# Layer 1's sums of squares for the sub-norm as two rounded products instead of one fp32 product

## The chip, the core and the metric

One core of a Trainium2 chip runs the whole program. The time is the device time of one execution in microseconds (us). The core has five engines that each work through a queue of their own in order: PE (TensorE, matrix products into PSUM), DVE (VectorE), ACT (ScalarE), POOL (GpSimd, which works on SBUF) and SP (SyncE, which here only issues transfers). They wait for each other by semaphores.

## What is computed

The program is a trunk of two layers over 2048 tokens with a width of 1024. Layer 0 has two attention mixers, layer 1 one differential attention with eight heads of width 128. The change lies in layer 1, behind the attention of a head:

```python
o = differential_attention(q1, q2, k1, k2, v, lam)
o = rms_norm(o, subln_g) * (1.0 - lambda_init)
y = (o.reshape(b, s, C_W) * jax.nn.silu(gate)) @ w_out
return x + y
```

with

```python
def rms_norm(x, g):
    xf = x.astype(jnp.float32)
    y = xf * lax.rsqrt(jnp.mean(xf * xf, axis=-1, keepdims=True) + EPS)
    return (y * g.astype(jnp.float32)).astype(x.dtype)
```

So for every token and head the 128 values of `o` are squared and summed, and the row is scaled by the inverse root of their mean.

## The kernel before

Every large product works with rounded operands (type `F32R` in the source; the trace calls it fp32r on what is written and f32 on what is read). A value is split into a high part, a copy into `F32R` on ACT, and a low part, the difference, on DVE or POOL; a product of two split operands is then three products (`mm3`, lines 214 to 216).

The kernel runs layer 0's projections (tiles named `p0...`), its mixing (`m...`), layer 1's projections (`p1...`), and layer 1's mixing (`c...`, `_mix1`). Layer 1's mixing takes the four blocks of 512 queries from the last to the first, and in each block the eight heads: 32 passes in all. I count them 0 to 31; heads 0 to 7 are block 3, heads 24 to 31 block 0. A pass has these parts:

- `scores` (line 880): products of queries and keys (`cS`, lines 901 and 902), a maximum on DVE (905), the exponential on ACT (908), then on POOL, and for every fifth chunk on DVE, the two softmaxes are scaled and joined (924 to 934).
- `values` (line 937): for each 128 keys, transposes of the probabilities on PE (`ctr`, 947), the split on ACT and DVE (950, 951), and three products into `cO` (954 to 956).
- `gate` (line 965), at the end of a head's values: SP loads the gate's values `g` (969), ACT copies the head's output out of PSUM into `o` (971) and squares it into `sq` (973), ACT makes the first two steps of the sigmoid from `g` into `sg` (975, 976), POOL multiplies `o` by `g` (977).
- `rest` (line 979), put off: it is kept in the list `normal` and run when the values of the next head have reached `kt == 2` (lines 957 to 959), for the last head by `leave`. PE sums the squares over the head's 128 values, which lie on the partitions, with a matrix of ones (`ms`, 981); ACT takes the logarithm (982), DVE joins it with the sigmoid's (983), ACT takes the exponential (984), DVE scales `o` (985). In blocks 3 and 0 `o` is split for the output projection at once (`split`, lines 1002 and 1003); in blocks 2 and 1 it goes out to memory (989) and is read back by `fetch` (1013).

Next to the heads runs the work of `side`: the products for the gates (`cG`), and the output projection of each finished block (`com`, `out_step`). `pace` weaves these streams together in the order in which the source issues them. From this the framework makes each engine's queue at build time with a planner: an instruction is put into its engine's queue when, in the planner's own reckoning, its inputs are there and its buffer is free, the earlier issued first. On the chip each queue is then worked through in that order.

A buffer comes from a pool by its tag: tiles with the same tag share a fixed number of places. Tag "g" of pool `sb` has two places (`bufs=2`); "sq" and "sg" have one each. The PSUM pool `ptr` has two places under tag "tr", for the transposes `ctr` and for `ms`.

Of the kernel before, what the change touches and what calls it, by code (L numbers as in the profile page):

```python
# [11 lines left out]
F32R = mybir.dt.float32r  # L12
AF = mybir.ActivationFunctionType
ALU = mybir.AluOpType
# [4 lines left out]
P = 128  # L19
# [4 lines left out]
BLK = NTB * P  # L24
# [7 lines left out]
def f32(ap):  # L32
    return ap.bitcast(F32)
# [52 lines left out]
class Trunk:  # L86
# [758 lines left out]
    def _mix1(self, es):  # L845
        nc, tc, a, s = self.nc, self.tc, self.a, self.s1
        n = "c"
# [8 lines left out]
        sb = pool("sb", 2)  # L856
# [5 lines left out]
        mm = nc.tensor.matmul  # L862
# [74 lines left out]
        def values(h, b, res):  # L937
            us = res["u"]
            O = pO.tile([P, BLK], F32, tag="O", name=n + "O")
            nkt = (b + 1) * NTB  # L940
            for kt in range(nkt):
                j0 = max(0, kt - b * NTB)
                wd = (NTB - j0) * P
                tp = ptr.tile([P, 512], F32, tag="tr", name=n + "tr")
                kk = (kt % 4) * P
                for j in range(j0, NTB):
                    nc.tensor.transpose(tp[:, (j - j0) * P:(j - j0 + 1) * P], us[j][kt // 4][:, kk:kk + P], self.ident)  # L947
                H = sb.tile([P, 512], F32R, tag="ptH", name=n + "ptH", bufs=3)
                L = sb.tile([P, 512], F32R, tag="ptL", name=n + "ptL", bufs=3)
                nc.scalar.activation(H[:, :wd], tp[:, :wd], AF.Copy)  # L950
                nc.vector.tensor_tensor(L[:, :wd], tp[:, :wd], f32(H[:, :wd]), ALU.subtract)  # L951
                o = O[:, j0 * P:]
                vH, vL = (v[:, kk:kk + P] for v in res["v"][kt // 4])
                mm(o, vH, H[:, :wd], start=(kt == 0), stop=False, skip_group_check=True)
                mm(o, vL, H[:, :wd], start=False, stop=False, skip_group_check=True)
                mm(o, vH, L[:, :wd], start=False, stop=(kt == nkt - 1), skip_group_check=True)  # L956
                if kt == 2:
                    while normal:
                        normal.pop(0)()
                yield wd / P  # L960
            gate(h, b, O)
# [3 lines left out]
        def gate(h, b, O):  # L965

            rows, tok = slice(h * P, (h + 1) * P), slice(b * BLK, (b + 1) * BLK)
            g = sb.tile([P, BLK], F32, tag="g", name=n + "gg")
            nc.sync.dma_start(g, s["g"][rows, tok])
            o = ot.tile([P, BLK], F32, tag="ot", name=n + "ot")  # L970
            nc.scalar.activation(o, O, AF.Copy)
            sq = sb.tile([P, BLK], F32, tag="sq", name=n + "sq", bufs=1)
            nc.scalar.activation(sq, o, AF.Square)
            sg = sb.tile([P, BLK], F32, tag="sg", name=n + "sg", bufs=1)
            nc.scalar.activation(sg, g, AF.Exp, scale=-1.0)
            nc.scalar.activation(sg, sg, AF.Ln, bias=self.one)
            nc.gpsimd.tensor_tensor(o, o, g, ALU.mult)

            def rest():
                ms = ptr.tile([P, BLK], F32, tag="tr", name=n + "ms")  # L980
                mm(ms, f32(self.ones), sq, start=True, stop=True)
                nc.scalar.activation(sq, ms, AF.Ln, bias=self.eps, scale=1.0 / P)
                nc.vector.scalar_tensor_tensor(sg, sq, 0.5, sg, ALU.mult, ALU.add)
                nc.scalar.activation(sg, sg, AF.Exp, scale=-1.0)
                nc.vector.scalar_tensor_tensor(o, o, self.sub, sg, ALU.mult, ALU.mult)
                if b in (0, NB - 1):
                    split(h, b, o)
                else:
                    nc.sync.dma_start(s["o"][rows, tok], o)
                ended.add((h, b))  # L990

            normal.append(rest)
# [7 lines left out]
        def split(h, b, o):  # L1000
            yH, yL = y_tile(b), y_tile(b)
            nc.scalar.activation(yH, o, AF.Copy)
            nc.gpsimd.tensor_tensor(yL, o, f32(yH), ALU.subtract)
            y[b][h] = yH, yL
# [214 lines left out]
```

## Time and profile before

| | |
|---|---|
| median of 3 runs | 2887.84 us (2879.25 to 2898.03) |
| profiled execution | 2891.3 us |
| its span, first to last instruction | 2889.4 us |
| mean granted PE clock | 0.979 |
| layer 1's mixing, from the first `gate` to the last | 1883.7 to 2853.7 us |

The profile is one execution. Times in it are microseconds from the span's start unless marked ns. A group row reads: line, engine, operation, output tile `<-` input tiles, shapes, `x` count, busy time in us, mean of one in ns, idle time of the engine just before, and what ended that idle time. A row of a tile or a source line reads: count, then shortest, median and longest duration in ns, then first and last start. A row of the chain reads: start, duration, engine, tile and line, and how many pieces were joined. A row of the timeline adds, in brackets, how long the engine had been idle before and what released it. PEld is the load of a product's fixed operand, which overlaps PE's products. Products are pipelined and their ends are modelled, so the distance from one start to the next says more of their cost than the duration of one.

### The profile page before, as it was taken

How to read it: one execution, taken by the hardware profiler on the slowest of the kernel's cores; microseconds unless marked ns; L12 is line 12 of the kernel's file. 1: busy time of each engine (PE TensorE's matmuls, PEld its weight loads, DVE VectorE, ACT ScalarE, POOL GpSimd, SP SyncE). 2: the span in 40 equal slices, each digit the busy share in tenths (PEclk: the TensorE clock that was granted, in tenths of full speed). 3: DMA queues.
4: the chain of work that ended last, by engine and by line, in shares of the span. 5: the costliest groups of instructions: out<-in, count | busy, mean ns of one | idle time of the engine just before them, and what ended most of it. 6: DMA issues, size and time to landing. Idle time of an engine off the chain costs nothing.

```text
span 2889.4 us, 45239 instructions
## 1 busy us (share of the span) xinstructions
PE 2709.6 (94%) x13704; PEld 2234.1 (77%) x13704; DVE 1955.8 (68%) x4874; ACT 1592.5 (55%) x4135; POOL 1588.1 (55%) x1740
## 2 busy tenths in 40 slices
PE   7999999998999998999999999989999999899898
PEld 5888888887788887777788887767777877677677
DVE  7752385257888885598638852667777888888742
ACT  4443543367676674343343322657667777777753
POOL 3541251335544453367645741667777887887841
PEclk9999999999999999999999999999999999999999
DMA  5673344649987874557884454776777787668772
GB/s 161 222 244 135 117 137 131 201 117 241 238 202 174 199 186 120 212 201 246 268 291 153 125 185 155 229 203 178 209 213 217 209 230 216 174 188 217 211 248 92
DMA packets 408868, 555.86 MB, mean 192 GB/s; under 512 B 47152, under 2 KB 187184, under 8 KB 408624
## 3 DMA queue, kind: packets, MB, share of 16 engines
q1 hardware_dynamic: 408624, 552.96, 65.4%
q8 instruction: 110, 1.80, 0.3%
q14 instruction: 134, 1.10, 0.1%
HBM read 388.18 MB, written 164.63 MB: 191 GB/s over the span
## 4 chain that ended last, share of the span: by engine, by line
PE 66%; DVE 11%; DMA 8%; ACT 4%; issue 3%; POOL 2%; SPq 1%; ACTq 0%; DVEq 0%; POOLq 0%
PE p1mm L216 5%; PE p1mm L214 5%; PE p1mm L215 5%; PE cS L901 3%; PE cS L902 3%; PE p0mm L216 3%; PE p0mm L215 3%; PE p0mm L214 3%; PE ctr L947 3%; PE cG L214 2%; PE cO L956 2%; PE com L214 2%; PE cG L215 2%; PE mom L214 2%; PE cG L216 2%
## 5 line engine op out<-in xcount | busy, mean ns | idle before, releaser
L908 ACT ACTIVATE cP<-cS,cnm 128x512 f32<-128x512 f32 (+3 forms) x640 | 398.7, 629 | 156.1 <-DVE cnm L905 99.2
L905 DVE TENSOR_REDUCE cnm<-cS 128x1 f32<-128x512 f32 (+3 forms) x640 | 374.8, 599 | 90.3 <-PE cS L902 86.1
L924 POOL TENSOR_SCALAR cP<-cP,crl,ce 128x512 f32<-128x512 f32 (+3 forms) x288 | 213.7, 755 | 248.8 <-DVE crl L919 74.5
L901 PE MATMUL cS<-ck,cqd 128*128 128x512 f32 (+3 forms) x640 | 263.0, 415 | 44.5 <-ACT cP L908 22.4
L215 PE MATMUL p1mm<-p1wL,p1hH 128*128 128x512 f32 x768 | 302.0, 393 | 0.4 <-POOL p1wL L310 0.4
L214 PE MATMUL p1mm<-p1wH,p1hH 128*128 128x512 f32 x768 | 301.7, 394 | 0.7 <-ACT p1wH L308 0.7
L216 PE MATMUL p1mm<-p1wH,p1hL 128*128 128x512 f32 x768 | 302.0, 394 | 0.0
L310 POOL TENSOR_TENSOR p0wL<-p0ws,p0wH 128x512 fp32r<-128x512 f32 (+1 forms) x124 | 149.0, 1232 | 270.5 <-ACT p0wH L308 260.5
L934 POOL TENSOR_TENSOR cP<-cP,cP 128x512 f32<-128x512 f32 (+3 forms) x256 | 288.6, 1148 | 0.5
L214 PE MATMUL p0mm<-p0wH,p0hH 128*128 128x512 f32 (+1 forms) x640 | 239.5, 376 | 4.7 <-ACT p0vt L472 3.3
L310 POOL TENSOR_TENSOR p1wL<-p1ws,p1wH 128x512 fp32r<-128x512 f32 x128 | 168.6, 1336 | 136.4 <-ACT p1wH L308 129.5
L902 PE MATMUL cS<-ck,cql 128*128 128x512 f32 (+3 forms) x640 | 236.5, 374 | 6.8 <-DMA cql<-qL 6.8
L216 PE MATMUL p0mm<-p0wH,p0hL 128*128 128x512 f32 (+1 forms) x640 | 239.6, 375 | 1.0 <-DVE p0hL L336 1.0
L215 PE MATMUL p0mm<-p0wL,p0hH 128*128 128x512 f32 (+1 forms) x640 | 239.2, 374 | 0.0
L951 DVE TENSOR_TENSOR cptL<-ctr,cptH 128x512 fp32r<-128x512 f32 (+1 forms) x320 | 190.3, 598 | 49.3 <-ACT cptH L950 48.5
L950 ACT ACTIVATE cptH<-ctr 128x512 fp32r<-128x512 f32 (+1 forms) x320 | 170.0, 538 | 57.8 <-PE ctr L947 57.4
L901 PEld LDWEIGHTS cS<-ck,cqd 128*128 128x128 f32 x640 | 123.2, 193 | 86.0 <-ACT cP L908 53.6
L933 POOL TENSOR_SCALAR cP<-cP,crl,ce 128x512 f32<-128x512 f32 (+3 forms) x231 | 178.0, 781 | 0.6 <-DVE crl L920 0.6
L947 PE MATMUL ctr<-ident,cP 128*128 128x128 f32 x1088 | 175.5, 277 | 1.5 <-DVE cP L931 0.5
L215 PEld LDWEIGHTS p1mm<-p1wL,p1hH 128*128 128x128 f32 x768 | 144.8, 188 | 29.7 <-POOL p1wL L310 0.8
L214 PEld LDWEIGHTS p1mm<-p1wH,p1hH 128*128 128x128 f32 x768 | 144.8, 189 | 29.6 <-ACT p1wH L308 1.0
L216 PEld LDWEIGHTS p1mm<-p1wH,p1hL 128*128 128x128 f32 x768 | 144.7, 188 | 28.8
(327 smaller groups left out, 7710.6 us busy)
## 6 DMA issues: line engine op xcount, KB each, us to landing
p1ws<-in_od_w_in_dram SPq DMA_DIRECT2D x56, 512.0 KB, 4.7
p0ws<-in_ev_w_in_dram SPq DMA_DIRECT2D x48, 512.0 KB, 4.5
ck<-kH SPq DMA_DIRECT2D x160, 128.0 KB, 4.0
ck<-kL SPq DMA_DIRECT2D x160, 128.0 KB, 4.2
cvH<-vH SPq DMA_DIRECT2D x80, 256.0 KB, 4.8
cvL<-vL SPq DMA_DIRECT2D x80, 256.0 KB, 4.4
cqd<-qH SPq DMA_DIRECT2D x128, 128.0 KB, 4.6
cql<-qL SPq DMA_DIRECT2D x128, 128.0 KB, 4.7
```

Of the source, the lines that this page charges most:

```text
L214: mm(ps, aH, bH, start=first, stop=False)
L215: mm(ps, aH, bL, start=False, stop=False)
L216: mm(ps, aL, bH, start=False, stop=last)
L310: low.tensor_tensor(l[:, :width], ws[:, k, :width], f32(h[:, :width]), ALU.subtract)
L901: mm(ps, qd[:, m, js], kt[:, :wd], start=True, stop=False)
L902: self.anchor = mm(ps, ql[:, m, js], kt[:, :wd], start=False, stop=True).ins
L905: nc.vector.tensor_reduce(nm[:, m, z:z + 1], ps, AX.X, ALU.max, negate=True)
L908: nc.scalar.activation(chunks[z][:, :wd], ps, AF.Exp, bias=nm[:, m, z:z + 1], accum_out=acc)
L924: nc.gpsimd.tensor_scalar(p1, p1, rl[:, 0:1], e1, ALU.mult, ALU.mult)
L934: nc.gpsimd.tensor_tensor(p1, p1, p2, ALU.add)
L947: nc.tensor.transpose(tp[:, (j - j0) * P:(j - j0 + 1) * P], us[j][kt // 4][:, kk:kk + P], self.ident)
L951: nc.vector.tensor_tensor(L[:, :wd], tp[:, :wd], f32(H[:, :wd]), ALU.subtract)
```

## The change

The squares are split as other operands are: `sH` is a rounded copy of `sq` made by ACT, `sL` is the difference `sq - sH` made by POOL. The sum is then two products of rounded operands, accumulated in the same PSUM tile, in place of one product of fp32 operands. The matrix of ones was already of the rounded type, and was read as fp32. Both new tiles have the tag "g", the tag of the gate's values, whose two places the three tiles now share.

```diff
             nc.scalar.activation(sg, g, AF.Exp, scale=-1.0)
             nc.scalar.activation(sg, sg, AF.Ln, bias=self.one)
             nc.gpsimd.tensor_tensor(o, o, g, ALU.mult)
+            sH, sL = (sb.tile([P, BLK], F32R, tag="g", name=n + "s" + part) for part in "HL")
+            nc.scalar.activation(sH, sq, AF.Copy)
+            nc.gpsimd.tensor_tensor(sL, sq, f32(sH), ALU.subtract)
 
             def rest():
                 ms = ptr.tile([P, BLK], F32, tag="tr", name=n + "ms")
-                mm(ms, f32(self.ones), sq, start=True, stop=True)
+                mm(ms, self.ones, sH, start=True, stop=False)
+                mm(ms, self.ones, sL, start=False, stop=True)
                 nc.scalar.activation(sq, ms, AF.Ln, bias=self.eps, scale=1.0 / P)
                 nc.vector.scalar_tensor_tensor(sg, sq, 0.5, sg, ALU.mult, ALU.add)
                 nc.scalar.activation(sg, sg, AF.Exp, scale=-1.0)
```

## The prediction, before the changed kernel was run

> **What bounds the kernel now.** I read the page first, then the busy time by stage, the chain of work, the waits, and last the rows of the lines of `gate` and `rest`. From the page:
>
> ```profile
> span 2889.4 us, 45239 instructions
> PE 2709.6 (94%) x13704; PEld 2234.1 (77%) x13704; DVE 1955.8 (68%) x4874; ACT 1592.5 (55%) x4135; POOL 1588.1 (55%) x1740
> PE 66%; DVE 11%; DMA 8%; ACT 4%; issue 3%; POOL 2%; SPq 1%; ACTq 0%; DVEq 0%; POOLq 0%
> ```
>
> PE is busy for 94% of the span and carries 66% of the chain that ends last; DVE carries 11%, ACT 4%, POOL 2%. The change lies in layer 1's mixing alone. Its stages, cut by the four query blocks (3, 2, 1, 0), in the busy time by window:
>
> ```profile
> core 0: us, PE busy (x) PEld busy (x) DVE busy (x) ACT busy (x) POOL busy (x), PEclk, DMA share, GB/s
> 1850.00:2262.00 412.00, 382.44 (x1875) 306.47 (x1874) 296.27 (x674) 281.87 (x772) 308.91 (x346) 0.98 0.74 204
> 2262.00:2544.00 282.00, 263.49 (x1330) 211.38 (x1328) 247.21 (x579) 212.33 (x597) 229.43 (x258) 0.98 0.70 201
> 2544.00:2743.00 199.00, 178.59 (x874) 140.57 (x872) 162.93 (x493) 147.93 (x439) 163.24 (x197) 0.95 0.80 212
> 2743.00:2857.00 114.00, 103.38 (x483) 81.68 (x481) 51.08 (x141) 59.39 (x141) 47.25 (x55) 0.96 0.60 187
> ```
>
> PE is busy 93%, 93%, 90% and 91% of the four, so it bounds all of them, but with 79 us of idle time in 1007 that other engines cause. DVE (88% and 82%) and POOL (81% and 82%) are close behind in blocks 2 and 1. This is what decides: time taken off PE pays, time put on DVE and POOL there may be charged.
>
> **What is removed.** `rest` runs once for each of 8 heads and 4 blocks, 32 times. Its product is one fp32 matmul in the source and two instructions in the trace. The row of its tile, and pieces of the chain (the first and the last of these pairs, and two runs of rounded products of the same 128x512 size):
>
> ```profile
> L981 PE MATMUL cms<-csq,ones x64: 590/592/1062, 1904.0 to 2853.6; 128*128 128x512 f32 x64
> ```
>
> ```profile
> 1904.20 0.86 PE cms L981 x2
> ...
> 2825.68 0.68 PE com L216 x3
> ...
> 2837.74 0.91 PE com L216 x4
> 2840.07 0.87 PE cms L981 x2
> ...
> 2845.54 0.86 PE cms L981 x2
> ...
> 2853.29 0.88 PE cms L981 x2
> 2854.19 0.70 ACT csq L982
> 2854.91 0.70 DVE csg L983
> 2855.64 0.64 ACT csg L984
> 2856.37 0.76 DVE cot L985
> 2857.15 0.64 ACT cyP L1002
> 2857.84 0.80 PE com L214
> ```
>
> The pair takes 0.86 us of the array. Rounded products follow one another every 0.23 us (0.68 / 3, 0.91 / 4), so the new pair takes 0.45 us. Saved: 0.86 - 0.45 = 0.41 us a head, 32 x 0.41 = 13.0 us of PE. How much of it is on the path? The chain holds a piece of this kind for 23 of the 32 heads, so I take 23 x 0.41 = **-9.4 us**; bounds 0 and -13.0.
>
> **What is added.** Per head one ACT copy into `sH` and one POOL subtraction into `sL`. The same two operations, with the same shapes, stand in `split`, and POOL's other two-input work beside them:
>
> ```profile
> L1002 ACT ACTIVATE cy<-coy 128x512 fp32r<-128x512 f32 x16 | 10.1, 630 | 10.1 <-DMA coy<-o 10.1
> L1003 POOL TENSOR_TENSOR cy<-cot,cy 128x512 fp32r<-128x512 f32 x8 | 10.4, 1296 | 7.9 <-ACT cy L1002 7.9
> L977 POOL TENSOR_TENSOR cot<-cot,cgg 128x512 f32<-128x512 f32 x32 | 41.6, 1299 | 27.8 <-ACT csq L973 27.7
> L934 POOL TENSOR_TENSOR cP<-cP,cP 128x512 f32<-128x512 f32 (+3 forms) x243 | 273.9, 1147 | 0.5
> ```
>
> ACT: 32 x 0.63 = 20.2 us. POOL: 32 x 1.30 = 41.5 us. Both run beside PE, and I charge an engine's new work at the rate at which its present work is on the chain. ACT's 4% of 2889.4 is 116 us out of 1592.5 busy, 7%: 20.2 x 0.07 = **+1.5 us** (bounds 0 and 20.2). POOL's 2% is 58 out of 1588.1, 4%: 41.5 x 0.04 = **+1.5 us** (0 and 41.5). If that cover goes (a block in which POOL is the last), its price is the whole 1.30 us a head.
>
> POOL's new work has a second price, on DVE. Rows of two DVE operations that read two inputs from SBUF, in the lines of the mixing window and by duration:
>
> ```profile
> L917 DVE TENSOR_TENSOR cpe<-ce,cla 128x6 f32<-128x6 f32 (+2 forms) x91 | 54.3, 597 | 19.2 <-ACT cP L908 13.9 <-ACT ce L916 4.9
> L983 DVE SCALAR_TENSOR_TENSOR csg<-csq,csg 128x512 f32<-128x512 f32 x32 | 34.7, 1086 | 17.4 <-ACT csq L982 17.4
> L917 DVE TENSOR_TENSOR cpe<-ce,cla x96: 141/168/3411, 1794.4 to 2687.0; 128x8 f32<-128x8 f32 x32, 128x6 f32<-128x6 f32 x32, 128x4 f32<-128x4 f32 x32
> L983 DVE SCALAR_TENSOR_TENSOR csg<-csq,csg x32: 664/693/5725, 1905.9 to 2854.9; 128x512 f32<-128x512 f32 x32
> ```
>
> Their means lie far over their medians: 91 x (597 - 168) ns = 39.0 us and 32 x (1086 - 693) ns = 12.6 us are lost to something. The longest L983 took 5.7 us. If POOL's two-input time is the cause (273.9 + 41.6 = 315.5 us of it), DVE loses 51.6 / 315.5 = 0.16 us for each us of POOL; 41.5 x 0.16 = 6.8 us of new DVE time. DVE's 11% of the span is 318 us of 1955.8 busy, 16%: 6.8 x 0.16 = **+1.1 us** (0 and 6.8).
>
> The Trainium skill, SBUF — State Buffer, section "Who interferes with whom", has this as a rule: a DVE instruction with two SBUF inputs contends with a GpSimd instruction that reads SBUF, the later of them waiting until the other is finished. The rows above agree in direction (141 ns alone at the least, 3411 at the most). By that rule each new subtraction could hold DVE up for as long as it runs, which is the rival C below; by the rows it is the 1.1 us.
>
> **What is moved: the wait for `sL`.** The second product can't start before POOL's subtraction, which stands behind `o*g` on POOL; behind the product stand, on PE, the next head's transposes and values. The nearest row is another low part on which a product waits:
>
> ```profile
> L956 PE MATMUL cO<-cptL,cvH 128*128 128x512 f32 (+1 forms) x320 | 126.1, 394 | 22.1 <-DVE cptL L951 18.3 <-DVE cl L918 3.1
> ```
>
> 18.3 us in 320, 0.057 us each; 32 x 0.057 = **+1.8 us**. Lower bound 0; the upper is the rival A. I take the row, because there too the wait is for the low half of a split on another engine.
>
> **What is moved: the load of `g`.** `sH` and `sL` take tag "g", which has two buffers. Before, head h+1's `g` could be loaded while head h's was in use. After, head h has `g` and `sH` in the two, `sL` takes the place of `g` once `o*g` is through, and the next `g` waits on SP until head h's product has read `sH`. Behind it on SP wait loads of keys, queries and values. The rows of the tile and of the tail:
>
> ```profile
> DMA to landing us min/median/max: 3.1/4.9/7.0
> ```
>
> ```profile
> 2844.98 1.28 POOL L977 TENSOR_TENSOR cot<-cot,cgg 128x512 f32<-128x512 f32 x1 [6.63 <-ACT csq L973]
> ...
> 2852.45 1.28 POOL L977 TENSOR_TENSOR cot<-cot,cgg 128x512 f32<-128x512 f32 x1
> ```
>
> While heads last 30 us and more, a load of 4.9 us after the product is early enough for the next gate; what it costs is that ACT, in order, may reach `exp(-g)` before it. Nearest row: ACT's waits for `coy`, loaded just ahead of use, 10.1 us in 16 loads; 31 x 0.63 = 19.6 us of ACT, at 7%: **+1.4 us** (0 and 19.6).
>
> The last two heads are closer together. Head 29's product ends at 2840.07 + 0.87 = 2840.94 in the chain, head 30's at 2846.40. `g` of head 30 would land near 2840.9 + 4.9 = 2845.8, 0.8 us after POOL now begins `o*g`. Its `sL` ends near 2845.8 + 2 x 1.3 = 2848.4; `g` of head 31 lands at 2853.3 instead of before 2852.45: 0.9 us late. Then head 31's own `sL` adds 1.3 us before the product, and in the end nothing covers it: from 2853.29 on the chain is that head alone. Tail: 0.9 + 1.3 = **+2.2 us** (1.3 without late loads; 2.2 + 2 x 2.1 = 6.4 with two loads of 7.0).
>
> **Sum.** -9.4 + 1.5 + 1.5 + 1.1 + 1.8 + 1.4 + 2.2 = +0.1 us. The profiled execution took 2891.3 us around its span of 2889.4, so 2891.4 by its own time; it stands 3.5 above the median of the three runs, 2887.84, and by the median the forecast is **2888 us**: no change.
>
> **Rivals.**
> A, slower: PE waits for `sL`. It is in place at heads where the product now runs ahead of `o*g`:
>
> ```profile
> 2365.61 1.02 PE L981 MATMUL cms<-csq,ones 128*128 128x512 f32 x2
> 2368.26 1.28 POOL L977 TENSOR_TENSOR cot<-cot,cgg 128x512 f32<-128x512 f32 x1
> ```
>
> Here `sL` would end at 2368.26 + 2 x 1.28 = 2370.8, 5.0 us after the second product's slot. By such a reckoning 15 of 32 heads are short, from head 10 (these rows) to head 31 (2852.45 on POOL, 2853.29 in the chain), by 33 us together. If every us is paid and the rest of the sum holds: 2888 - 1.8 + 33 = 2919. It decides from about 31 us on. Against it: the order of PE's queue is planned anew, and the product can be put later. The Trainium skill, TensorE: Matmul & The Clock Gate, section "The mechanism", says that matmuls keep strict order, so that a waiting product holds all behind it; no row here shows the contrary.
>
> B, faster: the tail and ACT cost nothing and all 13.0 us are on the path: 2887.84 - 13.0 + 1.3 = 2876. For: PE's 93%. Against: nine heads' products are not on the chain.
>
> C, DVE is held up by POOL: 41.5 us at the most instead of 1.1 if all of it were on the path, 2888 + 40 = 2928; at half, 2908. For: DVE's 88% in block 2. Against: DVE's main rows, reductions out of PSUM, are not of the two-input kind.
>
> D, `g` comes late at each of the 8 heads of block 0, where it would be on the chain with its 4.9 us: 2888 + 8 x 4.9 - 1.4 - 0.9 = 2925. Against: until head 29 the gap from one head's product to the next gate is longer than a load.
>
> E, the gain isn't there: freed PE time turns to idle time, 2888 + 9.4 = 2897.
>
> **Numbers.** Forecast 0.46, A 0.15 (a third of it near the full price), B 0.19, C 0.07, D 0.06, E 0.07. About 1%, 29 us, is what a measurement of this kernel can tell from no change. Over 1% slower, above 2917: a third of A, half of C, D, and a little of a replanned order that happens to be worse: 0.16. Over 1% faster, below 2859, would need more than twice what is removed: 0.05. Within: 0.79. The range reaches down to B less the 6 us by which the runs scatter (2870) and up to A at nearly full price (2914).
>
> **What would show it.** Product rows of 0.45 us a pair in the chain (removal); ACT +20 and POOL +41 us busy (additions); means of L917 and L983 up, with POOL on top of them (DVE); PE idle before the second product, ended by POOL (A); ACT idle before `exp(-g)`, ended by the load (D); the first product of the last head's output near 2860 instead of 2857.84 (tail). Wrong I am if blocks 2 and 1 change their length by over 10 us each.

## The result, and the profile after

The changed kernel takes 2932.69 us, the median of 6 runs (2920.03 to 2938.99), beside 2886.66 us (2877.86 to 2898.03) of the kernel before on the same chip: a ratio of 1.0149, with a 95% interval of 1.0126 to 1.0172. It is 1.5% slower. The forecast was 2888 us with a range up to 2914: the measured time lies above the range. Ratios here and below are of fast executions alone, and three executions, one of 5248 us and two of some 9298 us, are left out of them.

The profiled execution took 2930.3 us; before, 2891.3. The head of its page and the shares of the chain:

```profile
span 2928.5 us, 45274 instructions
PE 2722.3 (93%) x13704; PEld 2243.3 (77%) x13704; DVE 1972.7 (67%) x4874; ACT 1609.0 (55%) x4167; POOL 1624.5 (55%) x1772
PE 61%; DVE 12%; DMA 11%; ACT 5%; issue 2%; POOL 2%; SPq 1%; DVEq 0%; ACTq 0%; POOLq 0%
```

ACT is up by 16.5 us and POOL by 36.4 us, near the 20 and 41 of the additions. The span is up by 39.1. PE's share of the chain falls from 66% to 61%, and what grows is DMA (8 to 11%), DVE and ACT: the path goes through PE less often. These shares alone do not tell a fast kernel from a slow one: the fastest kernel below (2870.33 us) has PE at 62%, and one of the slower ones (2923.63 us) at 67%. The groups of the touched lines in layer 1's mixing, by line (busy us, mean ns, then idle time before and what ended it):

```profile
L917 DVE TENSOR_TENSOR cpe<-ce,cla 128x8 f32<-128x8 f32 (+2 forms) x96 | 57.7, 601 | 31.4 <-ACT cP L908 25.7 <-ACT ce L916 5.2
L980 POOL TENSOR_TENSOR csL<-csq,csH 128x512 fp32r<-128x512 f32 x32 | 41.4, 1293 | 1.0 <-ACT csH L979 0.5 <-POOL cot L977 0.3
L987 DVE SCALAR_TENSOR_TENSOR csg<-csq,csg 128x512 f32<-128x512 f32 x32 | 31.0, 968 | 17.0 <-ACT csq L986 16.6
L989 DVE SCALAR_TENSOR_TENSOR cot<-cot,sub,csg 128x512 f32<-128x512 f32 x32 | 30.4, 952 | 6.0 <-ACT csg L988 5.2 <-DMA cvH<-vH 0.8
L979 ACT ACTIVATE csH<-csq 128x512 fp32r<-128x512 f32 x32 | 20.5, 640 | 0.2
L985 PE MATMUL cms<-csL,ones 128*128 128x512 f32 x32 | 13.9, 435 | 0.8 <-POOL csL L980 0.7
L984 PE MATMUL cms<-csH,ones 128*128 128x512 f32 x32 | 13.8, 431 | 3.5 <-ACT csH L979 3.3
```

The new work has the size that was foreseen: the copy 640 ns, the subtraction 1293. The row to look at is L985: in 32 heads PE stood idle 0.8 us for the low half. PE does not wait for POOL. All the same it is idle more. Layer 1's mixing, from its first product of queries and keys to the end, takes 1140.1 us after and 1107.6 before (by the first record of `cS`), 32.5 more. PE's idle time in it, summed over the gaps between its records, is 110.5 us after 84.9. The other 6.6 us of the span lie ahead of the mixing, where the two kernels issue the same work; the mixing begins between 1776.8 and 1795 us in the kernels run here, whatever was changed in it.

The window by stages (the columns are those of the prediction's first window):

```profile
1850.00:2262.00 412.00, 384.80 (x1894) 310.72 (x1893) 298.81 (x678) 286.91 (x781) 313.50 (x349) 0.97 0.74 208
2262.00:2544.00 282.00, 255.64 (x1250) 202.87 (x1249) 236.18 (x543) 203.05 (x571) 230.63 (x257) 0.95 0.69 196
2544.00:2743.00 199.00, 175.40 (x879) 138.50 (x877) 166.53 (x485) 147.38 (x437) 163.69 (x194) 0.97 0.69 197
2743.00:2857.00 114.00, 93.70 (x433) 74.47 (x434) 54.87 (x165) 60.40 (x157) 63.02 (x76) 0.90 0.74 211
```

Block 3 (first row) loses nothing, PE works 384.8 us of it, before 382.4. From the second row on PE gets less done: 1250 products where 1330 stood. Two kernels at different points of their work can't be compared at the same clock time, so I cut at the heads' gates. Counted from the start of the mixing, the changed kernel is 2 us late at the gate of head 13, 23 at head 18, 20 at head 21, 35 at head 24, 27 at head 31 and 32.5 at the end. So there are two stretches that lose, heads 13 to 18 and heads 21 to 24, and the tail. The first two in windows, before:

```profile
2469.00:2611.00 142.00, 126.56 (x624) 97.65 (x623) 122.08 (x322) 106.91 (x310) 114.61 (x130) 0.96 0.71 193
2689.00:2753.00 64.00, 51.89 (x241) 39.35 (x239) 46.23 (x174) 46.79 (x139) 54.78 (x71) 0.88 0.82 219
```

and after:

```profile
2478.00:2641.00 163.00, 137.73 (x654) 105.38 (x652) 133.62 (x342) 114.36 (x332) 132.06 (x151) 0.93 0.64 186
2715.00:2794.00 79.00, 54.08 (x252) 41.54 (x250) 54.96 (x186) 50.79 (x147) 62.53 (x85) 0.86 0.82 215
```

The same five heads take 163 us, not 142: PE idle 25.3 us, not 15.4, and 211 ns a product, not 203, at a granted clock of 0.93, not 0.96. The three heads of the second pair take 79, not 64, with 24.9 us of idle time, not 12.1. In the first pair PE also took longer for a product, at a lower granted clock. In the second the clock fell from 0.88 to 0.86 and the time of a product did not change (215 ns in both), so the runs do not show that idle time as such makes products slower.

What does PE wait for in such a stretch? The list of its waits has no entry for POOL; two entries for ACT grew, and the one for DVE's low part of the probabilities fell from 11.7 to 6.7 us. From the window of heads 13 to 18 (who waits, for whom, us in total, times, longest), before:

```profile
PE cS L901 <- ACT cP L908: 1.3, 3, 0.6
PE cO L954 <- ACT cptH L950: 0.3, 1, 0.3
```

and after:

```profile
PE cS L901 <- ACT cP L908: 9.5, 9, 3.6
PE cO L954 <- ACT cptH L950: 6.4, 2, 6.0
```

The first is the scores' products, which wait for the softmax's exponential. Over the whole mixing this entry is no larger than before (21.1 us after, 22.4 before), so the loss sits in no one kind of wait. The longest wait shows the manner. The timeline of the changed kernel (start, duration, engine, line; in brackets the idle time before and what ended it):

```profile
2492.06 0.68 DVE L905 TENSOR_REDUCE cnm<-cS 128x1 f32<-128x512 f32 x1
2493.25 6.38 DVE L987 SCALAR_TENSOR_TENSOR csg<-csq,csg 128x512 f32<-128x512 f32 x1
2493.75 5.33 POOL L934 TENSOR_TENSOR cP<-cP,cP 128x512 f32<-128x512 f32 x5
2499.55 0.68 DVE L905 TENSOR_REDUCE cnm<-cS 128x1 f32<-128x512 f32 x1
2499.66 0.63 ACT L988 ACTIVATE csg<-csg 128x512 f32<-128x512 f32 x1 [7.67 <-DVE csg L987]
2500.20 1.06 ACT L950 ACTIVATE cptH<-ctr 128x512 fp32r<-128x512 f32 x2
2500.83 0.80 PE L954 MATMUL cO<-cptH,cvH 128*128 128x512 f32 x1 [5.96 <-ACT cptH L950]
```

The norm's first step on DVE, 0.69 us by its median, takes 6.38 while POOL runs five additions of the softmax. ACT's exponential (L988) waits for it, the copy of a transposed tile (L950) stands behind that in ACT's queue, and PE stands 5.96 us. The late product is not the norm's but the values'. But the kernel before has the same event:

```profile
2512.07 5.72 DVE L983 SCALAR_TENSOR_TENSOR csg<-csq,csg 128x512 f32<-128x512 f32 x1
2518.71 0.79 PE L956 MATMUL cO<-cptL,cvH 128*128 128x512 f32 x1 [4.87 <-DVE cptL L951]
```

So it can't carry the difference alone. Over the whole mixing the two-input operations L917, L931 and the norm's two take 188.4 us of DVE after and 183.5 before, 5 us more.

What did change is how late the norm ends. From the start of the gate's copy (L971) to the start of the scaled value (L989, before L985), a mean over the eight heads of each block, worked out from the records of the two lines:

| us, blocks 3, 2, 1, 0 | gate to first product of `ms` | gate to scaled value |
|---|---|---|
| before | 16.7, 5.6, 5.2, 5.5 | 22.6, 12.2, 11.5, 9.5 |
| after | 16.6, 6.5, 5.8, 6.1 | 22.9, 19.4, 20.1, 11.3 |

The high product starts as early as the fp32 product did, but the norm ends 7 to 9 us later in blocks 2 and 1, where POOL was busy 81 to 82% of the time before. POOL's subtraction starts a mean of 8.7 and 8.4 us after the gate in these two blocks and ends at 10.0 and 9.7; the low product starts another 2.9 and 5.2 us later, when its turn comes. In the 16 heads of these blocks 9 to 63 other records of PE stand between the high product and the low one. PE shows no wait for it because the planner, which reckons with POOL's subtraction, has put the low product so far back in PE's queue that the subtraction is there. **A planned wait is a later place in a queue, and the list of waits does not show it.** From here on the question is what the late norm costs, and why.

### The profile page after: what moved, and what is told of

Same layout as the page of the kernel before. It is cut to its first block, busy times and chain, and to the rows that moved or that the text cites. A ratio compares the mean times of both kernels' runs of the same rounds, so it can differ in the third digit from the quotient of the medians.

```text
span 2928.5 us, 45274 instructions
## 1 busy us (share of the span) xinstructions
PE 2722.3 (93%) x13704; PEld 2243.3 (77%) x13704; DVE 1972.7 (67%) x4874; ACT 1609.0 (55%) x4167; POOL 1624.5 (55%) x1772
## 4 chain that ended last, share of the span: by engine, by line
PE 61%; DVE 12%; DMA 11%; ACT 5%; issue 2%; POOL 2%; SPq 1%; DVEq 0%; ACTq 0%; POOLq 0%
PE p1mm L216 5%; PE p1mm L214 5%; PE p1mm L215 5%; PE cS L901 3%; PE p0mm L214 3%; PE p0mm L215 3%; PE p0mm L216 3%; PE cS L902 3%; PE ctr L947 2%; DVE cnm L905 2%; PE mom L216 2%; PE mom L214 2%; PE mom L215 2%; PE cG L214 2%; PE cG L215 2%
## 5 line engine op out<-in xcount | busy, mean ns | idle before, releaser
L901 PE MATMUL cS<-ck,cqd 128*128 128x512 f32 (+3 forms) x640 | 262.5, 413 | 40.4 <-ACT cP L908 21.1
L950 ACT ACTIVATE cptH<-ctr 128x512 fp32r<-128x512 f32 (+1 forms) x320 | 170.2, 538 | 61.9 <-PE ctr L947 61.0
```

Of the source, the lines that this page charges most:

```text
L901: mm(ps, qd[:, m, js], kt[:, :wd], start=True, stop=False)
```

## The experiments

The expectations name theories by letters. R: the shared places of tag "g" cost the time. W: PE waits for `sL`. L: the added work of ACT and POOL is on the path. P: it is the planner's new order, whatever its cause. In the later ones, B: `ms` holds its place in PSUM too long. H: the norm ends late, and its places in SBUF come free late.

Where a kernel needs a place for an extra tile, 0.5 KB is freed by loading two gains of layer 1 (`od_q_norm`, `od_k_norm`) into the first pool of layer 1. The control is that move alone, with the kernel before otherwise:

> The kernel before with only the gains of layer 1 loaded in layer 1's projection, as in the runs that needed room. All theories: within 5 us of before. What it differs by is to be taken off the other runs with that edit.

Measured: 2895.72 us, ratio 1.0016 [0.9999, 1.0032]. The move is worth about 0.2% (0 to 0.3% by the interval), and the ratios below that include it are to be read against 1.0016.

### The parts of the change

**The product alone.** The squares are written rounded and one rounded product sums them; the low part is left out, and nothing is added.

```diff
-sq = sb.tile([P, BLK], F32, tag="sq", name=n + "sq", bufs=1)
+sq = sb.tile([P, BLK], F32R, tag="sq", name=n + "sq", bufs=1)
-mm(ms, f32(self.ones), sq, start=True, stop=True)
+mm(ms, self.ones, sq, start=True, stop=True)
```

> The kernel before, with the squares written by ACT as rounded values and one rounded product of them; the low part is left out. Nothing is added to any engine, no tile is added, no wait is new; PE has 0.63 us less in each of the 32 passes, 20 us in all. R, W and L: faster than before, 2868 to 2880. P: anywhere, also slower than before.

Measured: 2870.33 us, ratio 0.9926 [0.9907, 0.9946]. That is 22 us saved (16 to 27 by the interval). One rounded product in place of the pair frees 0.86 - 0.23 = 0.63 us a head, 20.2 us in 32. By the interval that is more than the share of 23 heads, 14.5 us, and it may be all of it. It is the one kernel here that beats both, and it does not compute the low part.

**The added work alone.** The kernel before keeps its fp32 product, and copy and subtraction go into a tile that nobody reads. The subtraction does read `sq`, so the norm's logarithm, which overwrites `sq`, has to wait for POOL.

```diff
+sH = sb.tile([P, BLK], F32R, tag="sH", name=n + "sH", bufs=1)
+nc.scalar.activation(sH, sq, AF.Copy)
+nc.gpsimd.tensor_tensor(sH, sq, f32(sH), ALU.subtract)
```

> The kernel before with its fp32 product, and beside it ACT's copy of the squares and POOL's subtraction into a place of their own, read by nothing. R and W: as before, 2885 to 2895. L: 2925 or more, since all of the added work is there and none of the gain. P: anywhere from 2880 to 2930.

Measured: 2936.8 us, ratio 1.0150 [1.0128, 1.0172]. Over the control that is 39 us, without the new product and without the tag "g".

**The copy alone** (the first two of those lines):

> The kernel before with only ACT's copy of the squares added, read by nothing (gains moved for room, as in the dead split, which took 44 us). If the price is POOL's: within 5 us of before. If it is ACT's: 20 us or more over it. If it is the planner's new order: no telling, and the two parts needn't add up to 44.

Measured: 2891.09 us, ratio 1.0002 [0.9987, 1.0017]. By itself ACT's copy costs nothing that these runs can tell.

**The subtraction alone**, of two tiles that are there in any case:

```diff
+sH = sb.tile([P, BLK], F32R, tag="sH", name=n + "sH", bufs=1)
+nc.gpsimd.tensor_tensor(sH, sq, o, ALU.subtract)
```

> The kernel before with only POOL's subtraction added, read by nothing (of the squares and o, since there is no rounded copy; two inputs and the same size as before). If the price is POOL's: 35 us or more over before. If it is ACT's: within 5 us of it.

Measured: 2927.41 us, ratio 1.0114 [1.0092, 1.0136]. The larger part of the loss is POOL's: 28 us over the control, of the 39 of copy and subtraction together. Its PE idle time in the mixing is 107.1 us, and the norm ends 15.8 and 20.0 us after the gate in blocks 2 and 1.

**The changed kernel with a place of its own for `sH`**, so that the next gate's load waits for one tile less:

```diff
-sH, sL = (sb.tile([P, BLK], F32R, tag="g", name=n + "s" + part) for part in "HL")
+sH = sb.tile([P, BLK], F32R, tag="sH", name=n + "sH", bufs=1)
+sL = sb.tile([P, BLK], F32R, tag="g", name=n + "sL")
```

> The changed kernel, but sH has a place of its own, so that the load of the next g follows o*g again and not the product (room for it: the gains of layer 1's queries and keys are loaded in layer 1's projection instead of before). Theory R (the shared places of tag g cost the 45 us): back to 2875 to 2895. Theory W (PE waits for sL) and theory L (ACT's and POOL's new work is on the path): stays at 2925 to 2940. Theory P (the 43 us are the planner's new order, whatever the cause of it): anywhere from 2870 to 2940.

Measured: 2925.41 us, ratio 1.0108 [1.0093, 1.0123]. Beside 1.0149 of the changed kernel this is some 12 us less, 16 with the control taken off (with an uncertainty of 9), so the shared tag looks dear. The parts point the same way: 39 us for copy and subtraction less 13 for the product make 26, this kernel loses 27 over the control, and the changed kernel loses 43. A later pair does not bear it out (below), so the price of the tag is not settled.

**The same, with the subtraction on DVE** (`nc.vector` for `nc.gpsimd`):

> As the one before, with the subtraction for sL on DVE instead of POOL: 32 x 0.69 us more of DVE, 41 us less of POOL. R: as the one before within 10 us. L, if it is POOL: 20 us or more below the one before. W: below it too, since sL no longer stands behind o*g. P: no order among the two.

Measured: 2916.39 us, ratio 1.0084 [1.0060, 1.0108]. The norm ends at 16.0 us in both middle blocks, and PE's idle time is 99.0 us. Better than on POOL by the medians (the intervals touch), still slower than before: something costs here too, though POOL has no part in it. It can be the way back from DVE or DVE's 22 us more of work; this run does not tell them apart.

### Is it POOL's time?

**Fills in place of the subtraction**, of the same length in all:

```diff
+for wd in (512, 512, 256):
+    nc.gpsimd.memset(sH[:, :wd], 0.0)
```

> As the one before, but POOL's added work only writes and reads nothing: three fills of 512, 512 and 256 columns, some 1.3 us together by the 0.42 us of a fill of 384 columns in the trace. If DVE's two-input operations, held up while POOL reads, carry the price of POOL's work: 25 us or more below the dead subtraction. If it is POOL's time itself: within 10 us of the dead subtraction.

Measured: 2901.41 us, ratio 1.0028 [1.0011, 1.0046]. It tells nothing of the question: the fills depend on no input, and the planner put all 96 ahead of the mixing. The row of the tile, with the first and the last start at its end:

```profile
L984 POOL MEMSET csH<- x96: 311/525/532, 1742.0 to 1790.7; 128x512 f32 x64, 128x256 f32 x32
```

The second attempt ties them to the head by a copy of one column on ACT ahead of them:

```diff
+nc.scalar.activation(sH[:, 0:1], sq[:, 0:1], AF.Copy)
+for wd in (512, 512, 256):
+    nc.gpsimd.memset(sH[:, :wd], 0.0)
```

> POOL's fills again (write only, read by nothing, some 1.3 us a pass), now made to wait for a one-column ACT copy behind the squares, so that they stand where the subtraction would stand and not ahead of the mixing, where all fills of the run before were worked off. If what costs is that POOL reads beside DVE: 2890 to 2902. If it is POOL's time or the planner's order: 2915 to 2930, as the dead subtraction (2927).

```profile
L985 POOL MEMSET csH<- x96: 305/522/552, 1899.7 to 2865.4; 128x512 f32 x64, 128x256 f32 x32
```

Measured: 2901.03 us, ratio 1.0038 [1.0020, 1.0057]; against the control 0.2%. The fills stand in their heads now, add about as much to POOL (1621.7 us busy in all, 1624.5 in the changed kernel), and no step of the norm depends on them. The norm ends at 12.3 and 13.9 us.

**A quarter of the subtraction**, `sH[:, :P]` from `sq[:, :P]` and `o[:, :P]`, with the norm waiting for it as before:

> The dead subtraction on POOL with 128 of its 512 columns, read by nothing: about a quarter of its time. If its price goes with POOL's time: a quarter of the 32 us over the control with moved gains (2896), so 2900 to 2908. If it is the planner's order, which the new instruction changes whatever its size: no such proportion, 2885 to 2930.

```profile
L983 POOL TENSOR_TENSOR csH<-csq,cot 128x128 fp32r<-128x128 f32 x32 | 15.1, 473 | 0.5
```

Measured: 2923.63 us, ratio 1.0105 [1.0070, 1.0141]. The norm ends at 15.6 and 17.5 us. Over the control 15.1 us of POOL's time cost 26 us (14 to 37 by the intervals), where 41.4 cost 28; in proportion it would have been 10. The profiled executions differ more: the mixing is 18 us longer than the control's with the quarter, 41 with the whole, but that one was the fastest of the quarter's four. So the price goes neither with POOL's time nor, in proportion, with its reading beside DVE. What is left is that the norm depends on POOL.

**Less work on POOL.** In `COMB = 4` DVE takes every fourth chunk of the softmax instead of every fifth. The kernel before with it, then the changed kernel with it:

> The kernel before with the same setting. If POOL's time was not yet short before: 2890 to 2900, so that the setting helps only the changed kernel. If POOL was short already: below 2885.

> The changed kernel with every fourth in place of every fifth chunk joined on DVE: some 16 chunks less on POOL (16 x 1.9 us = 30 us), 16 x 1.0 us more on DVE. If POOL's time is what the change has run out of: 2900 to 2912, 20 us or more below the changed kernel. If DVE is held up or full: 2935 or more.

Measured: 2889.50 us, ratio 1.0000 [0.9980, 1.0019]; and 2926.69 us, ratio 1.0114 [1.0079, 1.0149]. POOL's 1604.8 us busy is 20 less than in the changed kernel; by the medians a quarter of the loss goes with it, but the intervals overlap.

### What does the late norm hold?

**The place in PSUM.** From the first product to the end of the logarithm, `ms` keeps one of the two places that the transposes need, 197 us over the 32 heads after and 70 before. If the products are swapped, `ms` takes its place only when the low half is there:

```diff
-mm(ms, self.ones, sH, start=True, stop=False)
-mm(ms, self.ones, sL, start=False, stop=True)
+mm(ms, self.ones, sL, start=True, stop=False)
+mm(ms, self.ones, sH, start=False, stop=True)
```

> The changed kernel with its two products swapped: the one of sL, which waits for POOL, first, the one of sH second. Theory B (between the first product and the logarithm, ms holds one of the two PSUM places of the transposes, and the wait for POOL makes that 197 us in all instead of 70): held for some 45 to 75 us, and 2875 to 2895. Theory H (the rest of the pass ends late, and its SBUF places come free late): 2920 to 2935, since the logarithm waits for sL as before. Theory L (the added work): 2920 to 2935.

> The same swap with a place of its own for sH (2925 before the swap). B: 2870 to 2895, and not above the swap alone by more than the 5 us of the moved gains. H and L: 2915 or more.

Measured: 2939.68 us, ratio 1.0157 [1.0127, 1.0186]; with a place of its own for `sH` besides, 2948.84 us, ratio 1.0194 [1.0165, 1.0223]. The hold did fall, to 50 and 54 us, and nothing was gained. That theory falls. With the products in this order the place of its own gained nothing: the two intervals overlap, and 0.2% of the difference is the control's. With the other order it gained 12 us or more. What the shared tag costs by itself stays open.

**The same from the other side**: POOL's dead subtraction reads other tiles, so that other steps of the norm wait for it. If it reads `o` twice, only the last step, the scaled value, has to wait; if it reads `sg` and `o`, the step after the logarithm waits too, but not the logarithm.

```diff
+nc.gpsimd.tensor_tensor(sH, o, o, ALU.subtract)
```

> The dead subtraction of full size on POOL, reading o twice and not the squares, so that the logarithm, which overwrites the squares, has not to wait for it. POOL's work, its reads and its place in the queue are those of the dead subtraction (2927). B: 2890 to 2905, held for about 72 us. L and H (o is still read before the last scaling): 2920 or more.

```diff
+nc.gpsimd.tensor_tensor(sH, sg, o, ALU.subtract)
```

> The dead subtraction reading sg, which DVE overwrites right behind the logarithm: the rest of the pass waits for POOL as in the slow runs, but after the logarithm, when ms has given up its place. B: 2890 to 2905, though the scaled o comes 15 us and more after the gate in blocks 2 and 1. H: 2920 or more.

Measured: 2911.30 us, ratio 1.0064 [1.0042, 1.0086], the norm's end at 13.7 and 16.8 us; and 2930.03 us, ratio 1.0128 [1.0096, 1.0159], the norm's end at 17.6 and 19.2. `ms` holds its place 71 and 69 us, as before. Of these two the one whose norm ends later is the slower, with the same work on POOL and no longer hold in PSUM. So it goes for all five kernels that add hardly more than work on POOL (fills in place, `o` twice, a quarter, the whole, `sg` and `o`): by the mean of the two middle blocks the norm ends at 13.1, 15.3, 16.6, 17.9 and 18.4 us, and they are 0.4, 0.6, 1.1, 1.1 and 1.3% slower.

**The places of the outputs.** `o` shares four places with the loads of the output projection and the copies of the gates' products. The profile after has one wait for them, with PE waiting 6.0 us behind it (rows of its waits on ACT and PE: who waits, for whom, us in total, times, longest):

```profile
ACT cot L971 <- DMA out_dram<-cxr: 3.2, 1, 3.2
PE cO L954 <- ACT cot L971: 6.0, 1, 6.0
```

A fifth place, in the changed kernel:

```diff
-ot = pool("ot", 4)
+ot = pool("ot", 5)
```

> The changed kernel whole, with a fifth place for the tiles that the gate's outputs share with the loads of o and x and the copies of G (the place is paid for by loading two gains into the first pool of layer 1, as in the control). The late end of the norm keeps such a tile longer: from the gate's copy to the scaled value, a mean of 20 us in the two middle blocks instead of 12. If it is the shortage of these places that makes the late end dear (the profile after shows one such case, a gate's copy that waits for the writing of an output tile, with a product behind it that waits 6 us), the time falls to 2885 to 2905 us. If the places don't matter and the late end costs by where its work lands in the queues of ScalarE and VectorE, it stays at 2920 to 2940 us. In between, by the size of the fall: both.

Measured: 2936.58 us, ratio 1.0152 [1.0132, 1.0172]. That wait is gone (the longest of its kind is 1.0 us) and the time is not. The places of `o` are not it.

### Is it the lateness as such?

The last run adds nothing and takes nothing away. The kernel before writes its norm later into the order:

```diff
-if kt == 2:
+if kt == (3, 6, 6, 2)[b]:
```

> The kernel before with nothing added and nothing taken away: the norm of a head (its product, Ln, Exp, the scaled value, and what follows) is only written later into the order, behind value step 6 of the next head in the two middle blocks and step 3 in block 0, where before it stood behind step 2. By the steps' pace that is some 8 us later in the middle blocks, where the changed kernel ends the norm 7 to 8 us later than before. If a late end of the norm costs by itself, wherever its work then lands, 2910 to 2935 us. If the loss comes from the waits for POOL's result, at which the queues that hold the norm's work stand, or from work that POOL does, this kernel has neither and stays at 2880 to 2900 us.

Measured: 2903.23 us, ratio 1.0050 [1.0032, 1.0068]. The norm ends 24.6 and 21.4 us after the gate in blocks 2 and 1, later than in the changed kernel (19.4 and 20.1), for a third of its loss. Its window of heads 13 to 18, the stretch that lost most:

```profile
2477.00:2629.00 152.00, 135.33 (x653) 102.10 (x652) 127.12 (x336) 110.55 (x321) 122.92 (x140) 0.97 0.69 194
```

152 us, between 142 before and 163 after, with PE idle 16.7 us (15.4, 25.3) and the clock at 0.97. Of two norms that end equally late, the one that was issued late costs 0.5%, the one that was issued early and then held up by POOL 0.9 to 1.5% (the control taken off where it is in). So lateness as such can be a part of the loss, and not all of it.

### What is shown, and what stays open

Shown: the larger part of the loss comes with the link from the added subtraction to the norm. A subtraction on POOL for which a step of the norm must wait costs 0.6 to 1.5% (the control's 0.2% included), a quarter-sized one 1.05%; POOL's time without that link costs 0.2% with an uncertainty of the same size, ACT's copy by itself nothing, and the rounded product gains 16 to 27 us for some 20 freed. All twelve kernels in which a step of the norm waits for the subtraction, on POOL or DVE, are 0.6 to 1.9% slower, and the seven without that wait are at 0.5% or less, so bad luck in the order alone is an unlikely reading. Not the cause: the hold in PSUM, the places of `o`.

Not shown is where 17 of the 43 us come from: the parts add up to 26, and the shared tag, the one thing left, was dear in one order of the products and not in the other. No run has POOL read in full with no step of the norm waiting for it, so of the 14 us over the control that the mildest link costs (1.0064) a part may be POOL's reading.

Not shown, too, is why a norm that was issued early and held up costs more than one issued late. Its steps hold the single places of `sq` and `sg`, but the norm that was issued late ends later still (24.6 and 21.4 us) and costs 0.5%, which speaks against these places as the main part; a second place for them was not tried. Its steps also stand in the queues of ACT and DVE at points that the planner chose by its own reckoning. Each edit has the planner make all queues anew, and how far the order differs does not tell the price: of the 4928 records of PE in the mixing, compared by their tiles, 751 fall outside the longest order shared with the kernel before for that kernel with `COMB = 4`, which loses nothing, 530 with the fills in place, 543 with the quarter-sized subtraction, and 8 in the control.

## Why the prediction was wrong

By its own steps:

- **The product, -9.4 us.** Right in its mechanism. The chain after has the second product as a piece of 0.25 us at most heads where it has one, and a pair of 0.86 stood there before:

```profile
2121.26 0.25 PE cms L985
...
2884.40 0.25 PE cms L985
```

  The share was too low: the run with the product alone saved 22 us where 20.2 were freed, so the term was nearer to its bound, -13.0.
- **ACT's copy, +1.5.** Right for the copy by itself: 0.02% with an interval of 0.15% to either side. With the subtraction behind it the copy makes 11 us more (39 against 28), probably because the subtraction then waits for it; if so, that belongs to the wait for `sL` below.
- **POOL's subtraction as work, +1.5.** Right as far as it goes: 1.0038 for the fills against 1.0016 for the control, about 6 us with an uncertainty of the same size.
- **DVE held up by POOL, +1.1, and rival C.** The rows that were to show it hardly moved: L917 from 597 to 601 ns, the norm's first step from 1086 down to 968. With 41.4 us more of POOL's reading, the two-input lines together took 5 us more. The full rival (40 us) is refuted by the quarter-sized subtraction, which reads a quarter and costs about as much. By the rule of the Trainium skill (SBUF — State Buffer, "Who interferes with whom") a DVE instruction with two inputs from SBUF and a GpSimd instruction that reads it hold each other up; the 6.38 us of L987 beside five of POOL's additions agree with that in direction, though the rule speaks of one instruction and this one lasted through five. The same event of 5.72 us in the kernel before says that the change did not bring it.
- **The wait for `sL`, +1.8, and rival A.** This is the step that failed. The sum took the price from what PE waits for `cptL`, 0.057 us a product, and counted only a wait that would show on PE. It does not show there:

```profile
PE cms L984 <- ACT csH L979: 3.3, 1, 3.3
PE cms L985 <- POOL csL L980: 0.7, 1, 0.7
```

  The text even said why, in the words on rival A: "the order of PE's queue is planned anew, and the product can be put later". It went no further. If the product is put later, so is all that follows it: the logarithm, two steps on DVE, an exponential, the output's way to the projection. The norm's end moved by 7 to 9 us in the two middle blocks, and no term stood for that. By the subtraction alone, 1.0114 against the control's 1.0016, this step is worth 28 us, and with the copy ahead of it 39 (1.0150), where 1.8 stood.
- **The late load of `g`, +1.4, and rival D.** The load does wait for the product on SP, and ACT for the load (before: 7.5 us in 2 waits):

```profile
SPq L969 <- PE cms L984: 32.6, 9, 8.2
ACT csg L975 <- DMA cgg<-g: 14.3, 6, 4.9
```

  6.8 us more on ACT, at the rate of 7% half a microsecond. A place of its own for `sH` gained 12 to 16 us in one order of the products and nothing in the other, so the runs set no price on this term; it may be far too small.
- **The tail, +2.2.** Mis-sized, by the same omission. The last head's piece of the chain, and the row of the subtraction:

```profile
2886.74 0.53 ACT csq L973
2887.30 0.64 ACT csH L979
2887.98 0.79 PE cms L984
...
2892.28 1.71 PE com L216 x4
2893.99 0.42 PE cms L985
2894.43 0.70 ACT csq L986
```

```profile
L980 POOL TENSOR_TENSOR csL<-csq,csH x32: 1254/1283/1615, 1904.9 to 2889.9; 128x512 fp32r<-128x512 f32 x32
```

  The squares are done at 2887.27. By an estimate an fp32 product could have followed at once and ended at 2888.1 (2887.27 and the pair's 0.86). The subtraction starts at 2889.9, is through at 2891.2, and the low product then stands in PE's queue behind products of the output projection until 2893.99: it ends at 2894.4, 6.3 us later. From head 31's gate to the end the changed kernel loses 5.8 us, not 2.2.

The numbers together: the chance for over 1% slower was 0.16, and its four ways were a third of A, half of C, D, and "a replanned order that happens to be worse". The one that came is none of these in its mechanism: not a wait on PE, but a chain of small steps moved back. The sentence at the end of the prediction, that it would be wrong if blocks 2 and 1 changed their length by over 10 us each, named the right place: from gate to gate, block 2 loses 17.5 us and block 1 18.0.

## What to carry to other kernels

Where queues are planned at build time, a new dependency need not show as a wait: it can show as everything behind it moved back. So price it from the end of the chain that it lengthens (measure from the trace when that chain ends now, add the other engine's answer and its queue), not from the waits of the engine that takes the result. And before a product is traded for work on two other engines, ask what the path from those engines back costs: here some 13 us of TensorE were saved, and the way through POOL cost 28 to 39, even for a quarter of the work 26.

## What the runs showed that was not expected

- A DVE operation of 0.69 us with two inputs from SBUF took up to 6.38 us while POOL ran additions without a pause (L987 at 2493.25), and PE stood 5.96 us at the end of it. Over the whole mixing the two-input lines hardly grew with 41.4 us more of POOL's reading: 188.4 us after, 183.5 before.
- The mean time of a product did not simply follow the granted clock from run to run. In heads 13 to 18 it was 211 ns at 0.93 after and 203 at 0.96 before, but 207 at 0.97 where the norm was only issued later.
- A product of fp32 operands is two instructions of 0.43 us each, a rounded one of the same size 0.23, by the starts. The gain of some 20 us was real (22 measured, 16 to 27); it is smaller than the price of the way over POOL, and the changed kernel, with two rounded products, keeps only some 13 of it.
